# A chunk scan by unit phases and the sequential scan instruction, in a one-core hybrid encoder layer

## The chip, the cores and the metric

The kernel runs on one core of a Trainium2 chip. The metric is the time of one execution on the device in microseconds (us). The kernel before was timed in three runs: 1526.7, 1527.67 and 1529.14 us, median 1527.67 us. One more execution was profiled. It took 1530.28 us.

A core has TensorE (PE, matmuls and transposes), VectorE (DVE), ScalarE (ACT), GpSimd (POOL) and SyncE (SP, which here only issues DMAs). Each engine runs its own queue in order and waits for others by semaphores.

## The reference

One layer over a sequence of 2048 tokens of width 1024. `h = RMSNorm(x)` is projected to q, k, v, z_attn, u_ssm, z_ssm and the gates. An attention branch and a state-space branch are each projected back, gated, merged, and a last projection, a residual and a norm follow. The change is in the state-space branch, a bidirectional diagonal complex recurrence in 32 groups of 16 channels, each with 64 states and two directions:

```python
for d in range(N_DIRS):
    lam = lax.complex(a_re[d], a_im[d])
    dt = jnp.exp(log_dt[d])[:, None]
    a_bar = jnp.exp(lam * dt)
    coef = (a_bar - 1.0) / lam
    b_bar = lax.complex(b_re[d], b_im[d]) * coef[..., None]
    bu = ...                         # u times b_bar: 64 complex inputs a token and group
    _, xs = lax.associative_scan(_scan_op, (a_el, bu), reverse=(d == 1), axis=0)
    y = y + Re(xs) c_re - Im(xs) c_im
```

## The kernel before, in words

TensorE works in fp32r, and each operand is split in a high part (a copy on ScalarE) and a low part (the difference). A product of two tensors is then three matmuls.

**The main stream.** After four blocks of u, k and v projections, a stream of 112 projections follows: for each weight column block (a *weight*) two projections of 512 tokens (`proj`, `mm3`, line 218), 24 matmuls of 512 columns each. `wnext` (line 205) splits the next weight while the current one is used: the high part on ScalarE (line 164), the low part on POOL in four instructions of 256 columns (line 156). Raw weights are loaded by SP into two buffers (`wload_to`, line 172).

**The side stream.** Everything else of this stage, first the chunk scan (`ssm`), then the attention, is a generator that is advanced a step at a time from inside the main stream: `turn` (line 116) adds half the rate to a credit and runs steps while the credit is positive. There are four turns in a projection (two from `mm3` itself, one from the `tick` in its middle, one from the `tick` after it), and the rate is 1.237 while the first 62 projections run. Engine queues get their instructions in this written order.

**The parameters** (`ssm_params`, line 433) are some 150 small VectorE instructions on 128 x 32 tiles, in the last block of the u, k, v projections: the powers of the step matrix up to 8 (line 590), eight squarings of them for the scan levels (lines 592 to 598), and the input weights (lines 609 to 614).

**The chunk scan** (`ssm`, line 618) cuts the 2048 tokens into 256 chunks of 8 tokens and works in eight batches of four groups. The 128 partitions hold 64 forward and 64 backward states. For each batch:
- `prep_w` and `prep_o` (lines 641, 644) make the tables of input and output weights on POOL, 24 instructions of 128 columns each (lines 636 to 638).
- `mats` (line 684) transposes the input weights and splits them into Wh and Wl (lines 698, 701, 692).
- `load_u` and `split_u` (lines 661, 673) bring u from DRAM and split it. One raw buffer serves both halves, and the load of the next half is issued when the last one is split.
- `inject` (line 746) makes the chunk inputs, 24 matmuls of 256 columns, and copies them to X with ScalarE.
- `scan` (line 760) is a complex scan over the 256 chunks on VectorE: levels with more than 64 pairs with 12 scalar_tensor_tensor instructions (lines 772 to 774), the ten others with four tensor_tensor instructions (lines 784 to 787), up to 512 columns, most of them strided.
- `zmat` (line 706) makes the matrix within a chunk (M), by matmuls (lines 722, 729), through DRAM.
- `hcopy` (line 804) splits the scanned states into Hh and Hl (lines 809, 811), and `emit` (line 813) makes the outputs of half a batch, 18 matmuls for each of two groups.

The order is set by cost: `scan` yields an estimate of its VectorE time, and whenever 0.994 us of it have been issued, one piece of the other work is issued and the step ends. `pieces` (line 849) lists that work: `mats` and `prep_o` of the next batch in the first step, `emit` of the batch before, then the second part of `mats`, `split_u` and `prep_w` of the batch after next, and so on. A batch has 16 steps.

Of the kernel before, what the change touches and what calls it, by code (L numbers as in the profile page):

```python
# [24 lines left out]
M = S // T  # L25
GB = 4
# [6 lines left out]
SCAN_SLOT = 0.994  # L33
FIRST = 1.711
# [4 lines left out]
def kernel(  # L39
# [382 lines left out]
    NLEV = 8  # L422
    lv_re = prm.tile([128, G, NLEV], F32, name="lv_re")
    lv_sw = prm.tile([128, G, 2, NLEV], F32, name="lv_sw")
# [8 lines left out]
    def ssm_params(pool):  # L433
# [181 lines left out]
        yield 4  # L615


    def ssm(pool):
# [10 lines left out]
        def table(i, tag, p_re, p_im, q_re, q_im, bufs):  # L629

            o = [pool.tile(sh, F32, tag=f"{tag}{n}", name=f"{tag}{n}", bufs=bufs) for n in range(2)]
            pr, pi, qr, qi = bc(p_re, i, 1), bc(p_im, i, 1), bc(q_re, i, 0), bc(q_im, i, 0)
            for n, (a, b, c, d, op) in enumerate(((pr, qr, pi, qi, ALU.subtract), (pr, qi, pi, qr, ALU.add))):
                for g in range(GB):
                    tmp = [pool.tile([128, T, C], F32, tag=f"t{m}", name=f"t{m}") for m in range(2)]
                    Q.tensor_tensor(tmp[0], a[:, g], b[:, g], ALU.mult)
                    Q.tensor_tensor(tmp[1], c[:, g], d[:, g], ALU.mult)
                    Q.tensor_tensor(o[n][:, g], tmp[0], tmp[1], op)
            return o

        def prep_w(i):
            st[i] = {"wt": table(i, "wt", wi_re, wi_im, bb_re, bb_im, 1)}

        def prep_o(i):
            st[i]["wo"] = table(i, "wo", wo_re, wo_im, cc_re, cc_im, 2)

        def split_o(i):
            st[i]["ws"] = [split(t, sh, f"ws{n}", 1) for n, t in enumerate(st[i].pop("wo"))]

        def sign_o(i):  # L650
            wo = st[i]["wo"]
            A.activation(wo[1], wo[1], AF.Copy, scale=-1.0)
            ncc = pool.tile([128, GB, C], F32, tag="ncc", name="ncc", bufs=2)
# [7 lines left out]
        def load_u(i, half):  # L661
            U = pool.tile([128, 2, M], F32, tag="u", name="u")
            for j in range(2):
                nc.sync.dma_start(out=U[:, j], in_=chan(uS, i * GB + half * 2 + j))
            raw_u[i, half] = U

        def split(raw, shape, tag, bufs):
            hi, lo = [pool.tile(shape, F32R, tag=tag + t, name=tag + t, bufs=bufs) for t in "hl"]
            A.activation(hi, raw, AF.Copy)
            V.tensor_tensor(lo, raw, hi.bitcast(F32), ALU.subtract)  # L670
            return hi, lo

        def split_u(i, half):
            u = raw_u.pop((i, half))
            st[i].setdefault("U", []).append(split(u, [128, 2, M], f"U{half}", 2))
            if half == 0:
                load_u(i, 1)
            elif i + 1 < NB:
                load_u(i + 1, 0)

        def split_m(i):
            st[i]["M"] = split(st[i].pop("m"), [128, GB, 128], "M", 1)

        def mats(i):
            g0 = i * GB
# [20 lines left out]
        def zmat(i):  # L706
            g0 = i * GB
# [3 lines left out]
            wo = s["wo"]  # L711
# [22 lines left out]
            yield  # L734
            Mt = pool.tile([128, GB, 128], F32, tag="M", name="M")
# [77 lines left out]
        def emit(i, half):  # L813
# [19 lines left out]
            if half == 1:  # L833
                st.pop(i)
# [803 lines left out]
```

## Time and profile before

| what | value |
|---|---|
| runs, median (lowest to highest) | 1527.67 us (1526.7 to 1529.14) |
| the profiled execution, its time | 1530.28 us |
| its span, first to last instruction | 1528.5 us |
| granted TensorE clock, mean | 0.975 |
| busy: TensorE, VectorE, ScalarE, GpSimd | 1423.8, 1027.4, 644.7, 629.1 us |

Busy time is summed over the instructions of an engine. Matmuls overlap in the records, so a matmul lasts longer there than the distance to the next one. "Idle before" is the time for which an engine had nothing to run, and the name behind it is what released it. In the rows, L755 is line 755 of the kernel. PEld is the weight load of TensorE, SPq and ACTq are DMA issues. Names of tiles stand as output<-inputs.

### The profile page before, as it was taken

Reading aid. Unit: us, or ns where it says so; the run is one execution under the profiler, and the core shown is the slowest. Engines: PE = TensorE matmul, PEld = TensorE weight load, DVE = VectorE, ACT = ScalarE, POOL = GpSimd, SP = SyncE. Lnnn points to the kernel's source line nnn. Section 1 sums busy time; section 2 is a strip of 40 time slices with the busy share of each in tenths; the row PEclk is TensorE's granted clock in tenths of the full one; section 3 lists DMA queues with packets and bytes.
Section 4 is the critical chain, followed back from the end, with each engine's and each line's share of the span. In section 5 each row is a group of like instructions: output and inputs, shape, how many; then the busy total and the mean of one; then the engine's idle time right before and its main releaser. Section 6 shows DMA issues by size and latency. Waiting matters only on the chain.

```text
span 1528.5 us, 20091 instructions
## 1 busy us (share of the span) xinstructions
PE 1423.8 (93%) x6933; PEld 1154.0 (75%) x6933; DVE 1027.4 (67%) x2145; ACT 644.7 (42%) x1165; POOL 629.1 (41%) x887
## 2 busy tenths in 40 slices
PE   7999959988899999799999999999988998999998
PEld 6787747767777777688878888888766786877886
DVE  3325607899889998927888988863577376386442
ACT  6332123343344434424666666654444143243111
POOL 5520366966777861723111111113367053153320
PEclk9999979999999999999999999999999999999999
DMA  7443212232232233454323233235576376375341
GB/s 263 152 109 89 77 62 87 85 98 87 74 106 94 89 100 97 148 153 133 94 87 94 90 101 94 89 111 154 179 205 183 120 186 180 111 187 182 111 125 69
DMA packets 240727, 185.51 MB, mean 121 GB/s; under 512 B 57921, under 2 KB 202433, under 8 KB 240625
## 3 DMA queue, kind: packets, MB, share of 16 engines
q10 hardware_dynamic: 108336, 100.61, 22.5%
q1 hardware_dynamic: 132288, 83.62, 18.4%
q8 instruction: 54, 0.88, 0.2%
q14 instruction: 49, 0.39, 0.1%
HBM read 126.56 MB, written 57.62 MB: 121 GB/s over the span
## 4 chain that ended last, share of the span: by engine, by line
PE 46%; DVE 19%; DMA 8%; POOL 6%; issue 5%; ACT 4%; ACTq 0%; SPq 0%; POOLq 0%; DVEq 0%
PE pj L221 9%; PE pj L223 9%; PE pj L222 9%; DVE Hl L811 3%; PE s L1484 3%; PE s L1485 3%; PE s L1486 3%; PE s L1055 2%; PE s L1002 2%; PE s L1039 2%; DMA yt<-yS 2%; POOL wl L156 2%; DMA ar<-aS 2%; DVE ft L784 1%; DVE fu L785 1%
## 5 line engine op out<-in xcount | busy, mean ns | idle before, releaser
L156 POOL TENSOR_TENSOR wl<-raw,wh 128x256 fp32r<-128x256 f32 x380 | 329.8, 899 | 597.8 <-ACT wh L164 586.2
L221 PE MATMUL pj<-hh,wh 128*128 128x512 f32 x976 | 395.4, 405 | 0.0
L223 PE MATMUL pj<-hh,wl 128*128 128x512 f32 x976 | 387.5, 397 | 5.3 <-POOL wl L156 5.3
L222 PE MATMUL pj<-hl,wh 128*128 128x512 f32 x976 | 386.8, 396 | 0.0
L223 PEld LDWEIGHTS pj<-hh,wl 128*128 128x128 f32 x976 | 186.5, 191 | 48.2 <-POOL wl L156 6.6
L221 PEld LDWEIGHTS pj<-hh,wh 128*128 128x128 f32 x976 | 187.6, 192 | 36.7 <-issue 3.6
L222 PEld LDWEIGHTS pj<-hl,wh 128*128 128x128 f32 x976 | 187.5, 192 | 33.8
L164 ACT ACTIVATE wh<-raw 128x1024 fp32r<-128x1024 f32 x96 | 100.7, 1051 | 19.9 <-DMA raw<-in_w_branch_ssm_dram 5.7
L1484 PE MATMUL s<-woh,mh 128*128 128x512 f32 x256 | 101.9, 398 | 6.4 <-DVE xr L1491 6.4
L1486 PE MATMUL s<-woh,ml 128*128 128x512 f32 x256 | 101.3, 396 | 0.0
L1485 PE MATMUL s<-wol,mh 128*128 128x512 f32 x256 | 101.2, 395 | 0.0
L405 ACT ACTIVATE st<-pj,bg 128x512 f32<-128x512 f32 x64 | 44.0, 687 | 98.7 <-PE pj L223 86.8
L1019 ACT ACTIVATE p<-p,sml 128x384 f32<-128x384 f32 (+1 forms) x128 | 75.8, 595 | 17.4 <-DVE sml L1015 17.4
L1042 ACT ACTIVATE ph<-s 128x512 fp32r<-128x512 f32 x92 | 54.3, 590 | 57.5 <-PE s L1039 57.5
L1528 POOL TENSOR_TENSOR sm<-sm,mhalf 128x1 f32<-128x1 f32 x15 | 8.3, 553 | 170.3 <-DVE sm L1527 133.7
L1003 DVE CUSTOM_DVE_ANT_0 p<-s,bias 128x384 f32<-128x384 f32 (+1 forms) x128 | 68.3, 533 | 12.6 <-PE s L1002 12.0
L1044 DVE TENSOR_TENSOR pl<-s,ph 128x512 fp32r<-128x512 f32 x92 | 63.2, 687 | 19.2 <-ACT ph L1042 17.8
L1491 DVE TENSOR_TENSOR xr<-xr,s 128x512 f32<-128x512 f32 x32 | 21.9, 684 | 68.9 <-PE s L1486 68.9
L1484 PEld LDWEIGHTS s<-woh,mh 128*128 128x128 f32 x256 | 48.1, 188 | 20.4 <-DVE xr L1491 9.1
L1002 PE MATMUL s<-kst,qs 128*128 128x384 f32 (+1 forms) x256 | 61.7, 342 | 0.6 <-issue 0.6
L1039 PE MATMUL s<-ident,p 128*128 128x128 f32 x368 | 57.6, 274 | 0.0
L1039 PEld LDWEIGHTS s<-ident,p 128*128 128x128 f32 x368 | 46.4, 140 | 14.7 <-DVE p L1031 2.2
(277 smaller groups left out, 3038.5 us busy)
## 6 DMA issues: line engine op xcount, KB each, us to landing
raw<-in_w_in_dram SPq DMA_DIRECT2D x59, 512.0 KB
gS<-st ACTq DMA_DIRECT2D x64, 256.0 KB
gt<-gS ACTq DMA_DIRECT2D x64, 256.0 KB
x<-in_x_dram SPq DMA_DIRECT2D x16, 512.0 KB
raw<-in_w_branch_attn_dram SPq DMA_DIRECT2D x32, 256.0 KB
raw<-in_w_branch_ssm_dram SPq DMA_DIRECT2D x32, 256.0 KB
out_dram<-xr ACTq DMA_DIRECT2D x15, 512.0 KB
xr<-in_x_dram SPq DMA_DIRECT2D x12, 512.0 KB
```

Source lines behind the costliest of these rows:

```text
L156: eng.tensor_tensor(lo[:, ks], r[:, ks], hi[:, ks].bitcast(F32), ALU.subtract)
L164: A.activation(res[0], r, AF.Copy)
L221: PE.matmul(pt, w[0][:, k], r[0][:, k], start=start and k == 0, stop=False)
L222: PE.matmul(pt, w[0][:, k], r[1][:, k], start=False, stop=False)
L223: PE.matmul(pt, w[1][:, k], r[0][:, k], start=False, stop=stop and k == kt - 1)
L1002: PE.matmul(pt[:, 0:w], s["qs"][:, h], kst[:, r, kv, k0 * 128:k1 * 128], start=r == 0, stop=r == 1)
L1003: V.tensor_tensor_reduce(out=p[:, h, 0:w], in0=pt[:, 0:w], in1=bias[:, kv * 4 + h, r0:r1:-1], scale=1.0, scalar=0.0, op0=ALU.add, op1=ALU. ...
L1019: A.activation(p[:, h, 0:w], p[:, h, 0:w], AF.Exp, bias=nm[:, j:j + 1], accum_out=den[:, j:j + 1])
L1039: PE.transpose(pt[:, h * 128:(h + 1) * 128], s["p"][:, h, i * 128:(i + 1) * 128], ident)
L1484: PE.matmul(pt, mh[k][:, ts_], wo[0, n][:, k], start=k == 0, stop=False)
L1485: PE.matmul(pt, mh[k][:, ts_], wo[1, n][:, k], start=False, stop=False)
L1486: PE.matmul(pt, ml[k][:, ts_], wo[0, n][:, k], start=False, stop=k == KD - 1)
```

## The change

The complex factor of the scan is split into its size and its phase. X is multiplied by the conjugate phases of its chunk number (`rotate`), after which the factor of every step is the real number rho. One sequential scan instruction for each group and each of the real and imaginary parts then runs over 255 chunks (`tensor_tensor_scan`), and a second rotation turns the states back. The phase tables are products of a 16-entry and an 8-entry table, made on POOL (`prep_e`) for one half and mirrored on ScalarE (`mirror_e`). X is cut in halves of two groups, with three buffers. Tables are made in instructions of 256 columns, those of batch 0 on VectorE. Raw u and M are loaded into the buffers of their low parts. The order is written out in `frame`, 18 steps a batch; the rates stay.

```diff
-        V.tensor_copy(lv_re[:, :, 0], pw_re[:, :, T])
-        lv_im = lv_sw[:, :, 1]
-        V.tensor_copy(lv_im[:, :, 0], pw_im[:, :, T])
-        for i in range(1, NLEV):
-            a = (lv_re[:, :, i - 1], lv_im[:, :, i - 1])
-            cmul(lv_re[:, :, i], lv_im[:, :, i], a, a)
-        ts(lv_sw[:, :, 0], lv_im, -1.0, None, ALU.mult, None)
...
+        e8 = ts(sm(), xr, 8.0, None, ALU.mult, None)
+        sc, e1 = exp_parts(e8)
+        stt(rho, e1, 1.0, sc, ALU.add, ALU.mult)
...
+        w = (cs, sn)
+        for _ in range(2):
+            cmul(cs, sn, w, w)
...
+        cmul(*lo(1), w, w)
+        def powers(re, im, n):
+            m = 2
+            while m < n:
+                a = (re[:, :, m // 2], im[:, :, m // 2])
+                cmul(re[:, :, m], im[:, :, m], a, a)
+                k = m - 1
...
+                tt(t_[0], x_[0], y_[0], ALU.mult)
+                tt(t_[1], x_[1], y_[1], ALU.mult)
+                tt(t_[2], x_[0], y_[1], ALU.mult)
+                tt(t_[3], x_[1], y_[0], ALU.mult)
+                tt(re[:, :, m + 1:2 * m], t_[0], t_[1], ALU.subtract)
+                tt(im[:, :, m + 1:2 * m], t_[2], t_[3], ALU.add)
+                m *= 2
+        def unit(re, im, n):
...
+        unit(el_re[:, :, 1:2], el_im[:, :, 1:2], 1)
+        powers(el_re, el_im, 16)
+        yield 4
+        cmul(*hi(1), lo(8), lo(8))
+        powers(eh_re, eh_im, 8)
+        unit(el_re, el_im, 16)
+        unit(eh_re, eh_im, 8)
+        yield 4
...
+        def product(o, p, q, eng):
+            for n, (a, b, c, d, op) in enumerate(
+                ((p[0], q[0], p[1], q[1], ALU.subtract), (p[0], q[1], p[1], q[0], ALU.add))
+            ):
+                for g in range(0, o[n].shape[1], 2):
...
+                    eng.tensor_tensor(tmp[0], a[:, gs], b[:, gs], ALU.mult)
+                    eng.tensor_tensor(tmp[1], c[:, gs], d[:, gs], ALU.mult)
+                    eng.tensor_tensor(o[n][:, gs], tmp[0], tmp[1], op)
...
+        def prep_e(i, half):
+            e = [pool.tile([128, 2, M], F32, tag=t, name=t, bufs=2) for t in ("ec", "es")]
...
+            product([t[:, :, 127:255].rearrange("p g (a b) -> p g a b", b=16) for t in e], p, q, Q)
...
+        def mirror_e(i, half):
+            for n, t in enumerate(ph[i, half]):
+                A.activation(t[:, :, 126::-1], t[:, :, 128:255], AF.Copy, scale=1.0 - 2.0 * n)
...
+        def rotate(i, half, back):
+            X = st[i]["X"][half][:, :, :, 1:M]
+            c, s_ = (t[:, :, 0:M - 1].unsqueeze(2).to_broadcast([128, 2, 2, M - 1]) for t in ph[i, half])
+            t = rtile()[:, :, :, 1:M]
+            V.tensor_tensor(t, X[:, :, ::-1], s_, ALU.mult)
+            V.tensor_tensor(X, X, c, ALU.mult)
+            for r in range(2):
+                V.tensor_tensor(X[:, :, r], X[:, :, r], t[:, :, r], ALU.add if r == back else ALU.subtract)
+        def scan(i, half):
+            X = st[i]["X"][half]
+            for j in range(2):
+                g = i * GB + half * 2 + j
+                for r in range(2):
+                    v = X[:, j, r, 1:M]
+                    V.tensor_tensor_scan(v, rho[:, g:g + 1].to_broadcast([128, M - 1]), v, 0.0, ALU.mult, ALU.add)
...
+        def frame(i):
...
+            inject(i, 0)
+            yield
+            inject(i, 1)
+            yield
+            rotate(i, 0, 0)
+            inject(i, 2)
+            yield
+            scan(i, 0)
+            inject(i, 3)
+            yield
+            if i == 0:
+                yield from zmat(0)
+                load_m(0)
+            rotate(i, 0, 1)
+            if nx:
+                next(ms)
+                prep_e(nx, 0)
+            yield
+            split_o(i)
+            if nx:
+                next(ms)
+                prep_o(nx)
+            yield
+            high_h(i, 0)
+            rotate(i, 1, 0)
+            if nx:
+                next(ms, None)
+            if nn:
+                prep_w(nn)
+            yield
+            low_h(i)
+            scan(i, 1)
+            yield
+            split_m(i)
+            rotate(i, 1, 1)
+            if nx:
+                prep_e(nx, 1)
+            yield
+            yield
+            yield from emit(i, 0)
+            yield
+            high_h(i, 1)
+            if nx:
+                mirror_e(nx, 0)
+                next(zs)
+            yield
+            low_h(i)
+            if nx:
+                split_u(nx, 0)
+                next(zs)
+            yield
+            if nx:
+                split_u(nx, 1)
+                mirror_e(nx, 1)
+                next(zs)
+            yield
+            yield from emit(i, 1)
+            if nx:
+                next(zs, None)
+            yield
+            if nx:
+                load_m(nx)
+            if nn:
+                load_u(nn, 0)
+                load_u(nn, 1)
+            st.pop(i)
+            yield
...
+        load_u(0, 0)
+        load_u(0, 1)
+        prep_w(0, V)
+        prep_e(0, 0)
+        prep_e(0, 1)
+        prep_o(0, V)
+        for _ in range(3):
             yield
         split_u(0, 0)
         split_u(0, 1)
         yield from mats(0)
+        mirror_e(0, 0)
+        mirror_e(0, 1)
+        load_u(1, 0)
+        load_u(1, 1)
         prep_w(1)
```

In the prediction, step s of a batch is the s-th stretch of `frame` that ends in a yield, counted from 1; `i` is the batch, `nx` the next one, `nn` the one after.

## Rows read from the trace of the kernel before

**Rows 1.** The page, busy time of the engines.
```profile
PE 1423.8 (93%) x6933; PEld 1154.0 (75%) x6933; DVE 1027.4 (67%) x2145; ACT 644.7 (42%) x1165; POOL 629.1 (41%) x887
```

**Rows 2.** TensorE's waits, 150 to 700 us: total us, times, longest.
```profile
PE s L825 <- DVE Hl L811: 26.8, 10, 5.2
PE s L755 <- ACT Wh L701: 17.5, 1, 17.5
PE s L825 <- ACT Hh L809: 7.7, 3, 6.1
PE pj L223 <- POOL wl L156: 5.3, 2, 3.1
PE s L755 <- ACT X L757: 2.8, 2, 2.7
```

**Rows 3.** Stretches: busy PE, PEld, DVE, ACT, POOL (instructions), clock, DMA share, GB/s.
```profile
228.40:277.60 49.20, 43.39 (x237) 34.67 (x236) 37.95 (x73) 17.07 (x28) 33.62 (x59) 0.97 0.22 73
...
540.90:589.70 48.80, 46.10 (x273) 37.82 (x272) 45.53 (x80) 22.58 (x33) 27.96 (x40) 1.00 0.29 89
```

**Rows 4.** Timeline of VectorE: start, duration, what; first, fifth and last of eight.
```profile
428.03 0.75 DVE L784 TENSOR_TENSOR ft<-X,lv_re 128x248 f32<-128x248 f32 x1
...
431.68 1.28 DVE L784 TENSOR_TENSOR ft<-X,lv_re 128x504 f32<-128x504 f32 x1
...
435.49 1.51 DVE L787 TENSOR_TENSOR X<-X,ft 128x504 f32<-128x504 f32 x1
```

**Rows 5.** Timeline of POOL, the same stretch.
```profile
428.37 9.10 POOL L156 TENSOR_TENSOR wl<-raw,wh 128x256 fp32r<-128x256 f32 x8
```

**Rows 6.** Single lines, whole run: shortest/median/longest ns, first to last start.
```profile
L811 DVE TENSOR_TENSOR Hl<-X,Hh x32: 1201/1316/1727, 287.8 to 660.0; 64x1024 fp32r<-64x1024 f32 x32
...
L670 DVE TENSOR_TENSOR Ml<-M,Mh x8: 678/792/1099, 260.7 to 625.7; 128x512 fp32r<-128x512 f32 x8
...
L772 DVE SCALAR_TENSOR_TENSOR X<-X,lv_re x64: 472/622/1018, 235.0 to 644.9; 128x256 f32<-128x256 f32 x32, 128x254 f32<-128x254 f32 x32
...
L156 POOL TENSOR_TENSOR wl<-raw,wh x380: 718/747/1790, 9.9 to 1466.8; 128x256 fp32r<-128x256 f32 x190
...
L636 POOL TENSOR_TENSOR t<-wi_re,bx_re x32: 401/404/1467, 179.8 to 520.3; 128x128 f32<-128x128 f32 x32
```

**Rows 7.** Timelines of TensorE, SP, POOL and ScalarE at the start of the scan.
```profile
186.30 0.60 PE L698 MATMUL s<-ident,wt 128*128 128x128 f32 x4
...
181.14 24.10 SPq L184 DMA_DIRECT2D raw<-in_w_in_dram  x2
...
202.07 2.77 POOL L156 TENSOR_TENSOR wl<-raw,wh 128x256 fp32r<-128x256 f32 x4
...
210.57 0.63 ACT L669 ACTIVATE U1h<-u 128x512 fp32r<-128x512 f32 x1 [22.96 <-DMA u<-uS]
```

**Rows 8.** Timeline of VectorE in the parameters.
```profile
136.05 0.42 DVE L492 SCALAR_TENSOR_TENSOR sm<-sm,sm 128x32 f32<-128x32 f32 x2
...
165.66 0.22 DVE L481 TENSOR_TENSOR sm<-lv_re 128x32 f32<-128x32 f32 x1
...
166.45 0.23 DVE L481 TENSOR_TENSOR sm<-lv_re 128x32 f32<-128x32 f32 x1
...
178.93 0.69 DVE L481 TENSOR_TENSOR bx_im<-tb,tb 128x512 f32<-128x512 f32 x1
```

**Rows 9.** Timelines of POOL, ScalarE and TensorE around one late low part.
```profile
398.06 0.58 POOL L636 TENSOR_TENSOR t<-wo_re,cc_re 128x128 f32<-128x128 f32 x1
...
408.74 1.05 ACT L164 ACTIVATE wh<-raw 128x1024 fp32r<-128x1024 f32 x1
...
429.38 0.50 PE L223 MATMUL pj<-hh,wl 128*128 128x512 f32 x1 [2.17 <-POOL wl L156]
...
429.72 0.40 PE L221 MATMUL pj<-hh,wh 128*128 128x512 f32 x1
429.96 0.40 PE L222 MATMUL pj<-hl,wh 128*128 128x512 f32 x1
```

More of the change, by code (lines that the diff above doesn't have):

```diff
@@ new lines, in rtile, with table, prep_w, prep_o @@
+        def rtile():
+            return pool.tile([128, 2, 2, M], F32, tag="rt", name="rt")
+        def table(o, i, p_re, p_im, q_re, q_im, eng):
+            pr, pi, qr, qi = bc(p_re, i, 1), bc(p_im, i, 1), bc(q_re, i, 0), bc(q_im, i, 0)
+            product(o, (pr, pi), (qr, qi), eng)
+        def prep_w(i, eng=Q):
+            o = [pool.tile(sh, F32, tag=f"wt{n}", name=f"wt{n}") for n in range(2)]
+            st[i] = {"wt": o}
+            table(o, i, wi_re, wi_im, bb_re, bb_im, eng)
+        def prep_o(i, eng=Q):
+            raw_o[i] = [pool.tile(sh, F32, tag=f"wo{n}", name=f"wo{n}") for n in range(2)]
+            table(raw_o[i], i, wo_re, wo_im, cc_re, cc_im, eng)
@@ L647, in split_o, with parts @@
+        def mirror_e(i, half):
+            for n, t in enumerate(ph[i, half]):
+                A.activation(t[:, :, 126::-1], t[:, :, 128:255], AF.Copy, scale=1.0 - 2.0 * n)
+        def parts(hi, lo, raw):
+            A.activation(hi, raw, AF.Copy)
+            V.tensor_tensor(lo, raw, hi.bitcast(F32), ALU.subtract)
+            return hi, lo
         def split_o(i):
[L648 removed]
+            st[i]["ws"] = [
+                parts(*(pool.tile(sh, F32R, tag=f"ws{n}{t}", name=f"ws{n}{t}") for t in "hl"), r)
+                for n, r in enumerate(raw_o.pop(i))
+            ]
@@ L804, in hcopy @@
-        def hcopy(i, half):
-            X = st[i]["X"]
-            gs = slice(half * 2, half * 2 + 2)
-            st[i]["H"] = H = [pool.tile([128, 2, 2, M], F32R, tag=t, name=t) for t in ("Hh", "Hl")]
-            for rows, xv in ((f, X[f, gs, :, 0:M]), (b_, X[b_, gs, :, M - 1::-1])):
+            if g % 2 == 0:
+                X = pool.tile([128, 2, 2, M], F32, tag="X", name="X", bufs=3)
+                s.setdefault("X", {})[g // 2] = X
+                V.memset(X[:, :, :, 0:1], 0.0)
+            X = s["X"][g // 2][:, g % 2]
@@ new lines, in inject @@
+            pt = bank("s1").rearrange("p (r m) -> p r m", r=2)
+            for n in range(2):
+                for m, (a, b) in enumerate(((0, 0), (0, 1), (1, 0))):
+                    PE.matmul(pt[:, n], s["W"][a][:, n, g], s["U"][g // 2][b][:, g % 2], start=m == 0, stop=m == 2)
+            A.activation(X[f, :, 1:M], pt[f, :, 0:M - 1], AF.Copy)
+            A.activation(X[b_, :, 1:M], pt[b_, :, M - 1:0:-1], AF.Copy)
+        def rotate(i, half, back):
[6 more added lines that the diff above has]
+                V.tensor_tensor(X[:, :, r], X[:, :, r], t[:, :, r], ALU.add if r == back else ALU.subtract)
@@ new lines, in scan, with high_h @@
+        def scan(i, half):
[5 more added lines that the diff above has]
+                    V.tensor_tensor_scan(v, rho[:, g:g + 1].to_broadcast([128, M - 1]), v, 0.0, ALU.mult, ALU.add)
+        def high_h(i, half):
+            X = st[i]["X"][half]
+            H = [pool.tile([128, 2, 2, M], F32R, tag=t, name=t) for t in ("Hh", "Hl")]
+            st[i]["H"] = H, ((f, X[f]), (b_, X[b_, :, :, ::-1]))
+            for rows, xv in st[i]["H"][1]:
@@ L809, in hcopy, with low_h @@
                 A.activation(H[0][rows], xv, AF.Copy)
-            for rows, xv in ((f, X[f, gs, :, 0:M]), (b_, X[b_, gs, :, M - 1::-1])):
+        def low_h(i):
+            H, xs = st[i]["H"]
+            for rows, xv in xs:
                 V.tensor_tensor(H[1][rows], xv, H[0][rows].bitcast(F32), ALU.subtract)
```

204 lines of the change are left out of this document (55 added, 149 removed).

## The prediction

> **What bounds the kernel now.** The page comes first: TensorE is busy 1423.8 of 1528.5 us [rows 1], so 104.7 us is all that anything but fewer matmuls could give, and the change removes no matmul. Next, who kept TensorE waiting between 150 and 700 us, where the chunk scan runs: 17.5 us once, for Wh; then 26.8 and 7.7 us for the copies of the scanned states (Hl, Hh), 5.3 us for a low part of a weight from POOL, 2.8 us for X [rows 2]. The last four, 42.6 us, belong to the eight batches; the 17.5 us is their start.
>
> Then the batches by stretch. From 228.4 us, where one batch's matmuls of L722 begin, to 589.7 us, where those of the seventh after it do, is 51.6 us a batch [rows 3]. VectorE is busy 45.53 of 48.80 us in the last of these, while TensorE has its own gaps: VectorE has hardly any slack here.
>
> Why VectorE is so busy is seen in the timeline of two engines side by side. From 428.03 to 437.0 us VectorE runs eight instructions and POOL eight low parts in 9.10 us [rows 4, 5], one for one. The durations say the same: Hl takes 1201 ns at least and 1727 at most, the low part of M 678 and 1099 [rows 6]. So an instruction of VectorE that reads two SBUF tensors is stretched by up to 0.53 us when POOL works. From 512 to 1024 columns the least duration rises by 523 ns, 1.02 ns a column: that is what VectorE needs for itself, the rest is fixed. The two engines take turns, and the stage is a sum over both.
>
> [...]
>
> **The change part by part.**
>
> *Pace of the batches.* A projection has four turns of 0.6185 credit, 2.474 steps. A batch had 16 steps, 6.47 projections; it now has 18, 7.28. A matmul of 512 columns goes every 0.23 us [rows 9], so a projection is 5.5 us; 46.10 us of TensorE work [rows 3] less 6.47 of them leaves 10.5 us for the batch itself. Without stalls a batch was 46 us and becomes 50.5 us, 2.8 us a step. The stage as a whole has 151 steps before (17 + 7 × 16 + 14 + 8) and 152 after (8 + 8 × 18), so attention starts beside the same projections: no cost there.
>
> [...] Before, VectorE: 12,736 columns of scan, 13 us at 1.02 ns and up to 17 as they are strided (L772 takes 472 ns for 256 columns [rows 6]); four Hl 4.2; five splits 2.6; 20 to 24 us. POOL: 48 table instructions of half the width of a low part, and 13 low parts, at 0.27 and 0.53: 20 us. Sum 40 to 44 us. After, VectorE: four rotations of two instructions of 1020 columns and two of 510, 12.5; eight scan instructions, Hl and splits as before, 6.8. The scan instruction stands in no row: at least a 256-column instruction (472 ns), at most a 512-column one (678), if each element costs two [rows 6]. I take 0.6, since each element needs the one before; the turn is then 0.26 to 0.52 us, 2.1 to 4.2 for eight. POOL: 24 table instructions of 256 columns, 12 more for the phase tables, 15 low parts, all at 0.53: 27 us. Sum 48.4 to 50.5 us. So the scan itself becomes cheap, but the rotations give the turns back and the phase tables add 6.4 us to POOL. The demand is 96 to 100% of the 50.5 us pace; before, it was 87 to 96% of 46.
>
> [...]
>
> *POOL's order.* Before, tables for wo were issued at a batch's second step and those for wt four later, so a low part could come between; still, the hi part of a weight at 408.74 us got its low part at 428.37, behind tables that began at 398.06, and TensorE waited 2.17 us [rows 5, 9]. Now the phases of the next batch's first half are issued at step 5, wo at 6, wt at 7, the second half's phases at 9. The first cannot start before the backward rotation has read the same buffer (two per tag). From step 3: rotation 3.5 us (1.2, 1.2, 0.68, 0.68 less overlap), scan 2.4, rotation 3.5: start at 9.4 us, step 6.4. Alone, instructions of 0.72 us then end the phases at 13.7, wo at 22.4, wt at 31, the last phases at 35.4. In turns with VectorE (17 more instructions, 12 us of turns until the second half is rotated back) wo ends at 31, wt at 40, the last at 44.5. A low part issued at step s stands behind all this and is needed one weight later, 4.95 steps or 13.9 us: issued at step 7 by 25.1, at 9 by 30.7, at 12 by 39. The wait is 0 to 6 us alone, 5 to 15 in turns, and every batch has one such weight; mean 3 and 10.5. I take **7 us** for each of the six batches that prepare all tables, 5 for the seventh (no wt), 3 for the eighth: 50 us in place of 42.6. Hl no longer waits: low_h stands two steps or more ahead of its matmuls; the low part of M, behind the second scan, may wait 0 to 4 us in the same stretch, and is covered by the wait for POOL.
>
> *The start.* Before, the load of the second half of u stood on the SP queue behind a load of weights that waited 24.10 us for a buffer, which POOL freed only after its tables, at 202.07 to 204.84; ScalarE waited 22.96 us for u and held up Wh [rows 7]. Now both loads of u are issued first: that wait goes. In its place come the parameters. They end at 179.6 us [rows 8]. Removed: seven complex multiplications at 0.79 us [rows 8], two copies, a negation: 6.6 us. Added: an exponential of 21 dependent instructions at 0.21, nine complex multiplications at 0.79, five blocks of six at 0.13 to 0.33, three normalisations of six (32, 256 and 512 columns, 7.6 us together): 25 us. They end at 198. The first transposes of wt come four steps earlier, at 177.5 instead of 186.30 [rows 7]; wt0 is ready at 201 to 203, since tables for batch 0 now go to VectorE while POOL makes phases. TensorE waits some 25 us, then 5 to 8 more until VectorE has made wo (12 instructions), both low parts of u and of W. That is 30 to 33 us against 17.5 and a few small ones: **+12 us**, between +6 and +18.
>
> *What costs nothing.* Each batch's u and M loads move to its end on the SP queue, behind nothing new; 14 and 9 steps (39 and 25 us) cover them, and without that cover the 22.96 us above shows the price. Four mirrors a batch go to ScalarE, 22.58 of 48.80 us busy [rows 3]. In-place low parts only save space.
>
> **Sum.** +12 at the start, +7.4 in the batches: 19.4 us. The profiled execution took 1530.28 us, span and 1.8 us around it; the median of the runs is 1527.67, 2.6 less. Against the median: **1547 us**.
>
> **Rivals.** *POOL keeps up (faster).* If low parts find POOL free, a batch loses 2 us, the last two 5 together: 17 instead of 42.6, with the start at +12 or +6: 1508 to 1514. For it: before, POOL made TensorE wait only twice, 5.3 us in all [rows 2]. Against it: the tables are now issued within five steps and their first is held to step 6.4. It decides at 13.9 us between the hi part of a weight and its low part. Chance 0.28.
> *Full turns (slower still).* 11 us a batch, 12 for the last two, the start at +18: 78 − 42.6 + 18 gives 1581. For it: the one-for-one stretch. Against it: VectorE has little of this work before step 3 and after the second backward rotation. Chance 0.14. [...]
> *The ends cancel.* Stalls of 5 us a batch and +6 at the start: 1529 to 1532, near no change. Chance 0.12.
> *My forecast*, 1535 to 1565: 0.46.
>
> **How the numbers follow.** A measurement here can tell about 0.2%, 3 us, from no change. Faster takes the first rival and a little of the third, 0.30; same, 0.08 of the third; slower, the rest, 0.62. The forecast's own range is 1535 to 1565; for 8 in 10 it must reach the middle of the first rival and the full turns: 1508 to 1582.
>
> **What would show it.** Right: TensorE waits of several us for wl in most batches, fewer for Hl; POOL above 85% busy between steps 6 and 16 of a batch; parameters ending near 198 us and a wait of over 20 us for wt behind them; rotation instructions of 1.2 us stretched to 1.7. Wrong: the hi parts of weights get their low parts within 10 us throughout, or the first transposes wait less than 15 us.

## The result, and the profile after

The changed kernel takes 1615.1 us, median of four runs (1613.59 to 1616.1); the kernel before took 1527.18 in four runs on the same chip. The ratio is 1.0573, with a 95% interval from 1.0554 to 1.0591: slower, as forecast, but by more than four times the 19.4 us of the sum, and outside the range (1508 to 1582).

The profiled span grew from 1528.5 to 1612.7 us, by 84.2. The page's line of busy times, which answers to [rows 1]:

```profile
PE 1433.5 (89%) x6933; PEld 1168.7 (72%) x6933; DVE 1007.9 (62%) x1940; ACT 654.9 (41%) x1197; POOL 692.4 (43%) x767
```

TensorE runs the same 6933 matmuls, but is busy 9.7 us longer, though no matmul was added; the other 74.5 us are waits. VectorE has less to do than before (1007.9 against 1027.4 us), POOL 63.3 us more. Who kept TensorE waiting from 150 to 800 us, the view of [rows 2], there up to 700 us (total us, times, longest):

```profile
PE s L872 <- DVE Ml L720: 64.9, 8, 10.5
PE pj L221 <- POOL wl L154: 34.8, 6, 8.5
PE s L767 <- issue: 22.7, 1, 22.7
PE s L829 <- DVE U0l L720: 4.1, 1, 4.1
PE s L767 <- DVE wt L686: 1.7, 1, 1.7
PE s L829 <- DVE Wl L761: 1.0, 1, 1.0
```

The first line has no counterpart before: the low part of the matrix M, made on VectorE, comes late in each of the eight batches. The second is the wait that the forecast rested on. The last four are the start, 29.5 us. The six come to 129.2 us, where [rows 2] came to 60.1: 69.1 more. With the 9.7 us of longer matmuls that makes 78.8 of the 84.2; the rest lies in waits outside this stretch and in gaps too short to be listed.

Two stretches of whole batches, from the first matmuls of `zmat` (line 792) in one batch to those in the next; `zmat` makes the matrix M, which the expectations below also call D (us, busy PE, PEld, DVE, ACT, POOL, then the granted clock, as in [rows 3]):

```profile
277.50:339.00 61.50, 54.08 (x301) 44.85 (x302) 38.76 (x44) 22.03 (x35) 39.38 (x42) 0.91 0.26 81
613.00:680.00 67.00, 53.29 (x295) 43.40 (x296) 40.54 (x41) 24.38 (x40) 50.68 (x55) 0.90 0.28 87
```

From 277.5 to 680.0 us is six batches, 67.1 us each, where [rows 3] gave 51.6. No engine is busy throughout: TensorE about 53 of 67 us, VectorE 41, POOL 51. So what sets the batch is no engine's amount of work alone but the order in which they wait for one another. One batch shows it. VectorE's timeline from the first half's turn back to M's low part, and then its idle stretches (in brackets, idle time before the instruction and what ended it):

```profile
442.18 1.57 DVE L838 TENSOR_TENSOR rt<-X,es 128x1020 f32<-128x1020 f32 x1
443.79 1.65 DVE L839 TENSOR_TENSOR X<-X,ec 128x1020 f32<-128x1020 f32 x1
445.47 2.02 DVE L841 TENSOR_TENSOR X<-X,rt 128x510 f32<-128x510 f32 x2
...
450.19 1.21 DVE L838 TENSOR_TENSOR rt<-X,es 128x1020 f32<-128x1020 f32 x1
...
455.65 2.77 DVE L862 TENSOR_TENSOR Hl<-X,Hh 64x1024 fp32r<-64x1024 f32 x2
458.43 3.99 DVE L850 TENSOR_TENSOR_SCAN X<-rho,X 128x255 f32<-128x255 f32 x4
462.34 1.14 DVE L720 TENSOR_TENSOR Ml<-Ml,Mh 128x512 fp32r<-128x512 f32 x1
...
486.42 0.28 DVE L800 COPY Z<-s 128x112 f32<-128x112 f32 x1 [6.42 <-PE s L792]
494.48 0.29 DVE L801 COPY Z<-s 128x128 f32<-128x128 f32 x1 [7.79 <-PE s L799]
...
502.86 1.22 DVE L838 TENSOR_TENSOR rt<-X,es 128x1020 f32<-128x1020 f32 x1 [7.80 <-ACT X L831]
```

TensorE over the same time; the transposes for the next batch's matrices (fifth and sixth step of this batch), the output matmuls (eleventh step), and what followed the two stalls:

```profile
441.70 0.60 PE L767 MATMUL s<-ident,wt 128*128 128x128 f32 x4
444.92 0.60 PE L767 MATMUL s<-ident,wt 128*128 128x128 f32 x4
...
456.30 0.28 PE L872 MATMUL s<-U0h,Mh 128*128 128x256 f32 x1
...
463.54 0.58 PE L872 MATMUL s<-U0h,Ml 128*128 128x256 f32 x1 [6.84 <-DVE Ml L720]
...
465.20 0.63 PE L219 MATMUL pj<-hh,wh 128*128 128x512 f32 x1
465.62 0.63 PE L220 MATMUL pj<-hl,wh 128*128 128x512 f32 x1
...
469.46 0.39 PE L220 MATMUL pj<-hl,wh 128*128 128x512 f32 x1
469.69 0.40 PE L221 MATMUL pj<-hh,wl 128*128 128x512 f32 x1
...
479.51 0.79 PE L221 MATMUL pj<-hh,wl 128*128 128x512 f32 x1 [6.53 <-POOL wl L154]
```

From the sixth step to the eleventh is 11.38 us, 2.28 us a step, for most of these steps carry no matmul of the batch. VectorE works without a pause from 442.18 on and is through with M's low part only at 463.48; TensorE wants it at 456.70. Later in the batch, from 480.0 us on, VectorE has next to nothing for 22 us (6.42 + 7.79 + 7.80), while TensorE does the second half's output and the next batch's injections. And TensorE stands a second time, 9 us after it got going, for a weight's low part. Its hi part was made at 450.28; POOL took up the low part at 478.25, behind a block of tables that began at 444.32 (timelines of ScalarE and POOL):

```profile
450.28 1.05 ACT L162 ACTIVATE wh<-raw 128x1024 fp32r<-128x1024 f32 x1
```
```profile
444.32 1.60 POOL L684 TENSOR_TENSOR t<-eh_re,el_re 128x256 f32<-128x256 f32 x1
...
478.25 2.35 POOL L154 TENSOR_TENSOR wl<-raw,wh 128x256 fp32r<-128x256 f32 x2
```

### The profile page after: what moved, and what is told of

It reads as the page before. It is cut to its first block, busy times and chain, and to the rows that moved or that the text cites. A ratio compares the mean times of both kernels' runs of the same rounds, so it can differ in the third digit from the quotient of the medians.

```text
span 1612.7 us, 19812 instructions
## 1 busy us (share of the span) xinstructions
PE 1433.5 (89%) x6933; PEld 1168.7 (72%) x6933; DVE 1007.9 (62%) x1940; ACT 654.9 (41%) x1197; POOL 692.4 (43%) x767
## 4 chain that ended last, share of the span: by engine, by line
PE 42%; POOL 14%; DVE 13%; DMA 6%; issue 6%; ACT 4%; ACTq 1%; SPq 0%; POOLq 0%; DVEq 0%
PE pj L221 8%; PE pj L219 8%; PE pj L220 8%; POOL t L684 4%; POOL t L685 4%; PE s L1562 3%; PE s L1563 3%; PE s L1564 3%; POOL wl L154 3%; PE s L1117 2%; PE s L1080 2%; PE s L1133 2%; DMA yt<-yS 2%; POOL wo L686 2%; POOL wt L686 1%
## 5 line engine op out<-in xcount | busy, mean ns | idle before, releaser
L154 POOL TENSOR_TENSOR wl<-raw,wh 128x256 fp32r<-128x256 f32 x380 | 340.9, 929 | 597.3 <-ACT wh L162 553.3
L221 PE MATMUL pj<-hh,wl 128*128 128x512 f32 x976 | 392.9, 403 | 34.9 <-POOL wl L154 34.8
L162 ACT ACTIVATE wh<-raw 128x1024 fp32r<-128x1024 f32 x96 | 100.8, 1052 | 22.3 <-DMA raw<-in_w_glu_dram 5.1
L838 DVE TENSOR_TENSOR rt<-X,es 128x1020 f32<-128x1020 f32 x32 | 44.2, 1380 | 56.1 <-ACT X L831 50.5
L1122 DVE TENSOR_TENSOR pl<-s,ph 128x512 fp32r<-128x512 f32 x92 | 63.4, 689 | 13.2 <-ACT ph L1120 12.1
L1080 PE MATMUL s<-kst,qs 128*128 128x384 f32 (+1 forms) x256 | 65.9, 338 | 0.0
L872 PE MATMUL s<-U0h,Ml 128*128 128x256 f32 x16 | 7.2, 447 | 64.9 <-DVE Ml L720 64.9
L862 DVE TENSOR_TENSOR Hl<-X,Hh 64x1024 fp32r<-64x1024 f32 x32 | 47.6, 1488 | 26.8 <-ACT Hh L857 26.5
```

Of the source, the lines that this page charges most:

```text
L154: eng.tensor_tensor(lo[:, ks], r[:, ks], hi[:, ks].bitcast(F32), ALU.subtract)
L162: A.activation(res[0], r, AF.Copy)
L221: PE.matmul(pt, w[1][:, k], r[0][:, k], start=False, stop=stop and k == kt - 1)
L1080: PE.matmul(pt[:, 0:w], s["qs"][:, h], kst[:, r, kv, k0 * 128:k1 * 128], start=r == 0, stop=r == 1)
```

## The experiments

All start from the changed kernel, which took 1615.1 us. e1 to e4, e6 and e10 were timed once, e11 in ten runs, the others in four. The *read weights* are the output weights (wo), the *write weights* the input weights (wt).

### One thing at a time

**e1: M's low part ahead of the second scan.**

```diff
             yield
+            split_m(i)
             low_h(i)
             scan(i, 1)
             yield
-            split_m(i)
             rotate(i, 1, 1)
```

> The low part of M is made before the low part of the states and before the second scan, instead of behind them; nothing else moves. Theory A (the order of VectorE's queue: TensorE's 64.9 us of waits for Ml are four scan instructions, four rows of about 1.0 us, that stand ahead of it): the wait for Ml goes, a shorter wait for Hl of about 3 us a batch takes its place, the eight waits fall from 65 to about 25 us together, time about 1570. Rival (VectorE is late by as much whatever comes last, because POOL stretches it): the wait only changes its name from Ml to Hl and stays above 50 us, time above 1600.

It took 1610.39 us beside 1527.02 for the kernel before. TensorE's waits:

```profile
PE pj L221 <- POOL wl L154: 57.1, 9, 13.3
...
PE s L876 <- DVE Hl L862: 18.6, 8, 2.7
PE s L792 <- ACT wo L731: 10.1, 2, 6.4
PE s L872 <- DVE Ml L720: 8.6, 5, 3.0
```

The wait for M went from 64.9 to 8.6 us, and 4.7 us came of it, for the rest came back under other names: 22.3 of it at POOL. In the batch shown above the two stalls were 6.84 and 6.53 us, the second over at 479.51. Here the same batch has almost nothing of the first, and the second is 12.14 us long and over at 479.12:

```profile
479.12 0.80 PE L221 MATMUL pj<-hh,wl 128*128 128x512 f32 x1 [12.14 <-POOL wl L154]
```

So the first stall had given POOL that time. The rival is right that the wait only changes its name, and in its time; but most of it went to POOL, not to Hl.

**e2: The phase tables of the first batch for all.** This leaves the other batches' tables out.

```diff
         def prep_e(i, half):
 
+            if i:
+                ph[i, half] = ph[0, half]
+                return
...
-            for n, t in enumerate(ph[i, half]):
+            for n, t in enumerate(ph[i, half] if i == 0 else ()):
```

> The phase tables are made for batch 0 alone and used by all batches: 84 POOL instructions and 28 ScalarE mirrors are left out, and the rotations of the other batches turn by the wrong phases. Theory B (turns with POOL stretch VectorE and hold back the low parts of weights): waits for wl from 34.8 to under 12 us, Ml from 64.9 to about 40, as half of the 12 instructions fall in the stretch before the low part of M, 0.5 us each; time about 1565. Rival (POOL's tables do not matter, only the order does): Ml stays above 58 us and the time above 1595. If the phase tables were the whole loss, the time would be near 1530.

1565.4 us, 49.7 less. The wait for POOL fell to 6.2 us, M's low part stayed late (line L723 is L720 of the changed kernel):

```profile
PE s L875 <- DVE Ml L723: 56.8, 8, 10.0
...
PE pj L221 <- POOL wl L154: 6.2, 3, 4.1
```

Theory B has the time and the wait for POOL right, its 40 us for M not. TensorE's busy time fell with the stalls, by 13.8 us to 1419.7.

**e3: The start.** The phase powers made on POOL (`qq` is its `tensor_tensor`), beside the rest of the parameters on VectorE; the first read weights after the first matrices; the low part of the main stream's second weight on VectorE.

```diff
-        prep_o(0, V)
         for _ in range(3):
...
         yield from mats(0)
+        prep_o(0, V)
...
-            tt(re, re, a, ALU.mult)
+                qq(re, re, a, ALU.mult)
```

> The phase powers go from VectorE to POOL, from the moment the sine and cosine are there, so that they run beside the other parameters; the output tables of batch 0 follow the split of u. Theory C (the 29.5 us of waits at the start are 25 us of small instructions in VectorE's queue): the first wait for wt falls from 22.7 to under 6 us, the start as a whole from 29.5 to under 10, time about 1590. Rival (the phases are needed anyway and the wait moves to the first batch): the first wait for Ml grows from 10 to 25 us or more and the time stays above 1605.

1606.78 us. The wait for the first write weights stayed as it was (24.3 in two waits, the longest 22.8, now put down to wt), the small ones behind it went: 5.2 us of the 29.5. The rival's bound (1605 or more) holds, though for another reason than it gave: the waits of the batches did not grow (M's low part 63.4, POOL 33.8). VectorE's timeline shows why the first weights came no earlier. It is through with its own parameters at 185.6 us and then stands until POOL has made the last of the powers:

```profile
197.32 0.43 DVE L703 TENSOR_TENSOR rt<-wi_re,bx_re 128x256 f32<-128x256 f32 x1 [11.70 <-POOL eh_im L600]
```

This first table instruction reads none of the powers. No run here shows what ties it to them, or what the start would take without that; the wait for the first weights is 22.7 or 22.8 us in every later kernel too.

**e4: POOL's tables apart.** The read weights' tables and their split go to the batch's first two steps, the phase tables to one step later on, the write weights' behind the first output.

```diff
             inject(i, 1)
+            if i:
+                mirror_e(i, 1)
+                if nx:
+                    prep_o(nx)
             yield
...
-                prep_e(nx, 0)
...
             yield
             if nx:
+                prep_e(nx, 0)
                 prep_e(nx, 1)
```

> The same work with POOL's tables and the splits of the output weights moved out of steps 5 to 9: output splits at step 1, output tables at 2, phase tables at 10, input tables at 12, mirrors in the next batch. Theory B: in steps 3 to 9 POOL has half as much to do and VectorE 2.2 us of splits less, so Ml falls from 64.9 to about 30 us and wl to under 20; time about 1560. Rival (total turns decide, not where they stand): the sum of waits for Ml, Hl and wl stays within 15 us of the 100 us it is now; time above 1600.

1576.15 us, 39 less, with nothing left out. The wait for POOL is gone, 0.6 us in one wait, and M's low part is as late as ever:

```profile
PE s L872 <- DVE Ml L720: 65.8, 8, 10.8
```

Theory B is right on POOL and wrong on M; the rival, who expected 85 us or more of these waits and over 1600 us, is wrong too.

### VectorE's order

**e6: M's and the first half's low parts first, the second half's rotations a step or two later**, on top of the tables apart; **e7**: the same with the new start.

```diff
             high_h(i, 0)
-            rotate(i, 1, 0)
...
+            split_m(i)
             low_h(i)
-            scan(i, 1)
+            rotate(i, 1, 0)
             yield
-            split_m(i)
-            rotate(i, 1, 1)
+            scan(i, 1)
...
+            rotate(i, 1, 1)
             yield from emit(i, 0)
```

> The spread of e4 (phase tables, split and read weights moved to other steps) with VectorE's steps laid out anew: M's low part and the low part of the first half's states go ahead of the second half's first rotation, the second scan follows a step later, and its turn back stands in the step before the output matmuls. e4 left TensorE 65.8 us of waits for M's low part (8 times) and 0.6 us for POOL; e1, with M's low part moved alone, left 8.6 us for it, 18.6 us for the states' low part and 57.1 us for POOL, in the same time. Theory C (two queues, POOL's and VectorE's, each able to hold a batch at about 64 us, so that mending one only hands the wait to the other; with both mended the waits go, and the slow matmuls behind each with them): 1520 to 1540, all three waits together under 25 us. Rival (VectorE and POOL share too much, so that whatever goes last is late by the same amount): 1565 to 1580, with 50 us or more under another name, the states' low part of either half.

> e6 with the start of e3 as well (phase powers on POOL beside the other parameters, the first read weights after the first matrices). Theory C: e3 alone gave 8 us, in a batch whose first waits were on VectorE's order; with that order mended the start should give 8 to 15 us more than e6, 1508 to 1530, below or level with the kernel before (1527). Rival (the start's wait only moves to the first batch): within 4 us of e6.

1575.63 and 1572.79 us, the second 1.0292 times the kernel before (1.027 to 1.0314). The start's share is 3 us, as the rival had it. M's low part is no longer late at all, 0.5 us in one wait, and nothing was gained by that. TensorE in e6 waits for this instead:

```profile
PE s L792 <- ACT wo L731: 50.7, 7, 9.6
```

ScalarE makes the sign of the read weights (wo) behind the second half's high part, which waits for VectorE's last turn back. So the wait, 50 us under another name as the rival had it, is for VectorE's queue once more, met at another place. In e7 VectorE is busy for some 44 us of a batch (414.62 to 458.66, with pauses of 4.3 us in all) and then, up to 476.30, idle for 16. One of e7's waits for the sign, and the low part that stands next on the way:

```profile
453.96 0.60 PE L811 MATMUL s<-wo,bx_im 64*32 64x112 f32 x8 [8.57 <-ACT wo L750]
```
```profile
452.20 2.90 DVE L881 TENSOR_TENSOR Hl<-X,Hh 64x1024 fp32r<-64x1024 f32 x2 [1.12 <-ACT Hh L876]
```

**e8: The next batch's first injections ahead of this batch's last output**, so that VectorE goes from one batch into the next; also the sign ahead of the high part, and the read weights' tables and their split at the batch's end. The diff is against e7.

```diff
-            inject(i, 0)
-            yield
-            inject(i, 1)
-            yield
-            rotate(i, 0, 0)
             inject(i, 2)
...
             rotate(i, 1, 1)
+            if nx:
+                next(zs)
             yield from emit(i, 0)
...
             high_h(i, 1)
-            if nx:
-                next(zs)
             yield
...
+            if nx:
+                inject(nx, 0)
+                mirror_e(nx, 0)
+                yield
+                inject(nx, 1)
+                mirror_e(nx, 1)
+                rotate(nx, 0, 0)
+                yield
             yield from emit(i, 1)
```

> e7 with the next batch's first two injections, and the turn of its first half, ahead of the output matmuls of this batch's second half (so a batch's rotation no longer waits for the batch before to be written out), and the sign of the read weights on ScalarE ahead of the second half's high part. In e7 VectorE is busy without a break for some 43 us of a batch (415.95 to 458.66) and then has nothing for 16 us, while TensorE does the second half's output and the next two injections; the waits have gone over to the matrix D (ScalarE wo 52.4 us, 7 times), which stands behind the second half's high part on ScalarE. Theory D (a chain through VectorE of 43 us plus the 16 us in which it has nothing sets the batch at about 57 to 60 us; the steps without matmuls of the batch, 2.2 to 2.3 us each, don't cover it): the 16 us go beside the chain, so 1515 to 1540, with less than 25 us of waits for D and the low parts together. Rival (VectorE beside POOL is full with 43 to 50 us a batch, and whatever is moved stretches it): over 1555, with 40 us or more of waits under new names.

1538.34 us, 1.0083 times the kernel before (1.0064 to 1.0103): 34.5 less than e7, with the same instructions. TensorE's waits in the batches:

```profile
PE s L848 <- ACT U0h L738: 14.5, 6, 3.3
PE s L848 <- DVE U0l L739: 12.8, 6, 3.8
PE pj L221 <- POOL wl L154: 8.3, 3, 4.0
```

The time is within theory D's numbers, and its waits for the sign and the low parts are gone but for 1.4 us of Hl. What is late is what the batch's first injection needs: the parts of the next inputs, which stand behind the same high part.

The new place of the injections and that of the sign are both in this run, and no run has either alone. In the batch of e7 shown above TensorE asks for the sign at 445.39 and first needs the second half's Hl at 462.13; Hl is there at 455.10. The work from the sign to Hl takes 8.2 us as recorded, and an estimate of 5.4 with its slow matmuls 0.23 us apart instead of 0.42 (both spacings from the last section). By this estimate an earlier sign alone would have left some 1.5 to 4.3 us of the 8.57 to wait. So a good part of the 34.5 us may be the sign's.

### What is left: POOL

**e9: Those parts early**, beside the matrices; **e10**: the same **with one set of phase tables**, the edit shown in e2.

```diff
                 next(ms)
+                split_u(nx, 0)
             yield
+            split_m(i)
             high_h(i, 0)
             if nx:
                 next(ms, None)
+                split_u(nx, 1)
             yield
-            split_m(i)
             low_h(i)
...
-                split_u(nx, 0)
                 next(zs)
...
-                split_u(nx, 1)
                 next(zs)
```

> e8 with the parts of the next batch's inputs (ScalarE high, VectorE low) made in the frame's sixth and seventh step instead of behind the second half's high part, and M's low part a step earlier. In e8 TensorE still waits 27.3 us for the first input's parts (U0h 14.5, U0l 12.8, 6 times each), since ScalarE stands at the second half's high part until VectorE has turned it back. Theory D: these waits go and nothing takes their place, so 1538 less 20 to 30 is 1508 to 1518, ahead of the kernel before (1527). Rival (VectorE full, a wait moves on to the low parts of the states): 1530 to 1540.

> e9 with the phase tables of the first batch used for all (84 POOL instructions and 28 mirrors of ScalarE left out, so batches 1 to 7 are turned by the wrong phases). In the changed kernel leaving them out gave 49.7 us. Theory D (the tables were dear only because of where they stood in POOL's order and since they stood in a chain; laid out with room they lie beside other work): within 8 us of e9. Rival (POOL's added instructions slow VectorE's by taking turns with them, wherever they stand): 20 to 50 us below e9.

1535.31 us (ratio 1.0062, 1.0041 to 1.0083) and 1482.2 us. Both of theory D's numbers were missed. In e9 the waits for the inputs went, and the wait for POOL took most of their place, where the rival, right in its time, had the low parts of the states (9.5 us):

```profile
PE pj L221 <- POOL wl L154: 30.5, 7, 11.3
```

Stretches of the two kernels over the stage (columns as in [rows 3]), the second without the tables:

```profile
230.00:700.00 470.00, 423.25 (x2305) 346.76 (x2305) 322.61 (x329) 193.64 (x298) 370.31 (x378) 0.96 0.34 102
```
```profile
230.00:700.00 470.00, 460.95 (x2550) 383.27 (x2550) 362.64 (x443) 213.43 (x340) 322.91 (x310) 0.99 0.37 114
```

POOL, 370.31 of 470 us busy, gives way to a TensorE that is busy 37.7 us longer in the same stretch. So leaving the tables out is worth 53 us here, no less than the 49.7 in the changed kernel.

**e11: POOL's tables in pieces of three instructions, one a step.**

```diff
+        def pieces(i):
...
+                for k in ks:
+                    prep_o(nx, ks=k)
+                    yield
...
+            for _ in frame(i, work):
...
+                        next(todo, None)
+                yield
```

> e9 with POOL's three tables of a batch issued in pieces of three instructions, one piece a step, instead of twelve to twenty-four at once; nothing is left out. In e9 TensorE waits 30.5 us for POOL's low parts of the side weights (7 times, up to 11.3 us); at 421.86 to 447.45 POOL works off 24 table instructions without a break while eight low parts stand behind them, and TensorE then waits 8.58 us. Leaving 12 of the 36 table instructions out (e10) gave 53 us. Theory E (order: the low parts are late because of the blocks ahead of them, POOL has room, 370 us busy of 470): 1495 to 1512, under 10 us of waits for POOL. Rival F (amount: POOL and VectorE together are full, each instruction of the one stretching the other's, so it is the number of table instructions and not their place): 1525 to 1540, with 25 us or more of waits for POOL, VectorE or ScalarE.

1525.39 us, ratio 0.9988 (0.9975 to 1.0001): level with the kernel before. 10 us came of the order, but 27.5 us of waits for POOL stayed:

```profile
PE pj L221 <- POOL wl L154: 27.5, 6, 8.9
```

These are rival F's numbers, by which what remains is the amount of POOL's work.

**Phase tables on VectorE**: in e12 the second half's, where VectorE waits for the next injection; in e13 both halves'.

```diff
                 inject(nx, 0)
                 mirror_e(nx, 0)
+                prep_e(nx, 1, eng=V)
                 yield
```

> e11 with the phase tables of a batch's second half made on VectorE (six 256-column instructions, 0.43 to 0.73 us each by the start's own tables on VectorE) where it stands waiting for the next batch's injection, 27.4 us in 6 waits in e11, instead of on POOL. POOL's own take 1.0 to 1.3 us each in this stage. Rival F of e11 (POOL's amount of work beside VectorE's, 387 us busy of 470): POOL is rid of 6 to 7 us a batch, VectorE takes 3 to 4 of them in a gap, so 20 to 30 us less than e11: 1497 to 1508, waits for POOL under 10 us. Theory E (POOL's order alone, or VectorE's chain): 1520 or more.

> e11 with the phase tables of both halves on VectorE, the first half's in the step of the second matrices. If the amount of POOL's work is what is left (F), 1485 to 1505, near e10 (1482, no such tables at all); if VectorE's chain binds next, 3 to 5 us a batch come back as waits for the low parts of M or of the states and it is no better than e12 or worse, 1505 to 1530.

1511.83 us, ratio 0.9899 (0.9879 to 0.992), and 1509.67, ratio 0.9882 (0.9859 to 0.9906). Neither leaves anything out, and both beat the kernel before, by 15 and 17 us. The waits of the first, then of the second:

```profile
PE pj L221 <- POOL wl L154: 16.9, 5, 5.1
```
```profile
PE s L898 <- DVE Hl L884: 18.8, 9, 3.9
```

The first gave 13.6 us where F expected 20 to 30, with 16.9 us of waits for POOL left. In the second POOL is not waited for any more, but VectorE's chain is, by some 2 us a time where 3 to 5 a batch were expected; the ranges of the two times overlap. That is the second expectation's other branch. The choice between POOL and VectorE is then even. That leaves 27 us between e13 and e10, the kernel without the tables, and no run here splits those between VectorE's added instructions, the 28 mirrors on ScalarE and the order, which e10 has from e9.

## Why the prediction was wrong

**The step that failed** is the last clause on POOL's order: "the low part of M, behind the second scan, may wait 0 to 4 us in the same stretch, and is covered by the wait for POOL". It waits 8.1 us a batch (64.9 in 8), and nothing covers it. Two things were wrong in it.

- *Its size.* The steps were priced at the batch's mean, 2.8 us. Those between the second injections and the output have hardly a matmul of the batch and last 2.28 us, so TensorE came to M at 14.6 us after the fifth step began (441.70 to 456.30), not at 6 × 2.8 = 16.8. VectorE needed 21.3 us from 442.18; by the least durations of these instructions (last section) it is some 16, which would have been some 1.5 us late already; the other 5 us are what these instructions took longer while POOL worked beside them. A mean pace may not stand for the steps in front of a deadline.
- *Its cover.* Two waits of TensorE cover one another only when they are for the same moment. These are 16 us apart (456.70 and 472.98), so both are paid. What M's wait does is to give POOL its length to catch up: this is why the wait for POOL, forecast at 50 us, was 34.8, and why it is 57.1 when M is moved ahead. The 50 us was near the truth for a kernel without the other stall.

**The second miss** is the clock, which was not priced at all. After twelve of the fourteen stalls of the batches TensorE runs at a granted clock of 0.50 for 3.5 to 5.9 us, its matmuls of 512 columns 0.42 us apart (last section). Behind the shortest, 2.58 us for POOL, it does so from 421.84 to 424.82 us, 0.9 us after it went on; behind the next, 3.00 us for POOL, its clock stayed at 1.00. Its busy time grows by 9.7 us. The kernel before had such stretches too: between 150 and 800 us 70 of its projection matmuls last 0.56 us or more, 115 of the changed kernel's.

By terms, measured against [rows 2]: start 29.5 − 17.5 = +12.0 (forecast +12; the kernel before had 2.5 us more of small waits there that [rows 2] leaves out, which makes it +9.5); POOL, Hl, Hh and X, 34.8 − 42.6 = −7.8 (forecast +7.4); M, +64.9 (forecast nothing of its own); longer matmuls, +9.7 (not priced).

**What held.** The parameters end at 197.4 us (forecast 198), TensorE stands 22.7 us for the first weights and then 6.8 in three short waits (forecast 25 and 5 to 8). Hl no longer waits. POOL is busy without a break from 444.32 past 478.25, and the one weight a batch whose hi part falls into that waits, six times. The scan instruction takes 656 ns at its shortest for 255 elements, near the upper end of its bounds; a plain instruction of 510 columns takes 682. So it spends about two columns' time on an element. With the upper end, 0.68 us in place of 0.6 for each of the eight, the sum would have been 0.6 us a batch higher: not the cause.

**The rivals.** POOL keeping up was the faster one, with "17 instead of 42.6" us. With the tables laid apart POOL does keep up (0.6 us), and the kernel is still at 1576: the rival would have needed VectorE's chain as well. *Full turns* put the whole excess on POOL, 1581; this number was the nearest, its mechanism not the one: POOL's waits came to 34.8 us, not 78.

**What the experiments showed of the cause.** The wait for M's low part is a symptom: removed alone it gives 5 us, removed after POOL's nothing. That the order in VectorE's and POOL's queues made the loss is shown: with nothing left out, other orders and the new start took the time from 1615 to 1525 us. What sets the batch once POOL's tables are apart is, by the timelines, a loop through VectorE: injection, rotation, scan, rotation back, low part, output, and the next injection only behind that output, so that VectorE's work and its idle time stand one behind the other (44 and 16 us in e7). The edit that breaks this loop gave 34.5 us together with the earlier sign; the loop's own share is argued, not shown. POOL's tables are the other half: 39 us came from laying them apart, 10 more from small pieces, 14 to 16 more from moving them. With all of that the kernel with the unit-phase scan is 1.0 to 1.2% faster than the kernel before. That the scan as such is faster is not shown, for no run gave the kernel before, with its own 42.6 us of waits in the batches, an order mended in the same way.

## What to carry to other kernels

Walk each in-order queue up to each deadline with the pace of the steps that actually stand before it, not with the stage's mean, and let one wait cover another only if both end at the same moment. When a wait that is moved away leaves the time as it was, look for the loop: which engine's idle time and busy time follow on one another from one batch to the next; starting the next batch's first step ahead of this one's last is then worth a try, alone, so that its share is seen. And instructions on the engine with "room" (POOL, 27.96 of 48.80 us busy [rows 3]) cost most of their length while they stood in blocks, since what queued behind them had a due time: without the phase tables POOL was busy 62.5 us less, and the kernel took 49.7 less (e2).

## What was not expected of the hardware

**Half speed after a stall.** Behind the stall of 6.84 us the projection's matmuls of 512 columns start 0.42 us apart (465.20, 465.62), until 469.46, then 0.23 (469.69). The granted clock is 0.50 from 463.50 to 469.40 us and 1.00 from 469.50 to 475.50. By these spacings the 6 us after the stall cost about 3 more, an estimate. Over a batch the granted clock is 0.90 or 0.91 where [rows 3] had 0.97 to 1.00. In the fastest version TensorE is busy 1414.9 us, 8.9 less than before, for the same 6933 matmuls.

**VectorE and POOL overlap in part.** Single lines over the whole run of the changed kernel (shortest, median, longest ns):

```profile
L720 DVE TENSOR_TENSOR U1l<-U1l,U1h x8: 684/1106/1211, 214.5 to 681.8; 128x512 fp32r<-128x512 f32 x8
...
L850 DVE TENSOR_TENSOR_SCAN X<-rho,X x64: 656/1032/1218, 226.4 to 728.4; 128x255 f32<-128x255 f32 x64
...
L838 DVE TENSOR_TENSOR rt<-X,es x32: 1203/1224/1751, 222.2 to 730.5; 128x1020 f32<-128x1020 f32 x32
...
L839 DVE TENSOR_TENSOR X<-X,ec x32: 1220/1523/1648, 223.5 to 731.7; 128x1020 f32<-128x1020 f32 x32
...
L841 DVE TENSOR_TENSOR X<-X,rt x64: 682/1102/1233, 225.2 to 733.6; 128x510 f32<-128x510 f32 x64
...
L862 DVE TENSOR_TENSOR Hl<-X,Hh x32: 1203/1552/1735, 250.7 to 742.2; 64x1024 fp32r<-64x1024 f32 x32
...
L684 POOL TENSOR_TENSOR t<-eh_re,el_re x16: 614/728/1600, 197.6 to 677.2; 128x256 f32<-128x256 f32 x16
...
L686 POOL TENSOR_TENSOR es<-t,t x16: 722/792/1766, 201.6 to 683.4; 128x256 f32<-128x256 f32 x16
```

From 443.79 to 463.97 us, 20.2 us, VectorE ran 18 instructions and POOL 16. By their shortest durations (for the two low parts of W, which read PSUM, the 0.68 us that they took) that is 14.8 and 10.4 us, 25.2 together, and 23.8 without those two. So each is stretched by the other (the scan from 656 to about 1000 ns, a POOL product from 614 to 1600), and yet they don't exclude one another for whole instructions. Beside POOL the rotation back took 1.57, 1.65 and 2.02 us (from 442.18 on, the last figure for two instructions); with nothing on POOL, from 730.50 us on, it took 1.21, 1.22 and 1.29.
